# A decoder layer on one core: the second product's blocks begun together and its end split by token half, the fourth product in 256-column matmuls, the last block finished in halves

## The chip, the cores and the metric

One Trainium2 chip, one core of it. The metric is the device time of one execution of the whole kernel in microseconds (us), lower is better.

## The reference

One decoder layer on 256 tokens of width 2048, in float32:

```python
u = jnp.einsum('bsd,dc->bsc', x, w_in[l])                       # 1st product, 2048 -> 6160
conv_out = conformer_conv_group(u[..., :CONV_CH], ...)          # gated, depthwise conv of 31 taps, LayerNorm, silu
gdn_out = gated_deltanet_group(...)                             # 8 heads of 128, chunked delta rule, RMS norm, gate
mix = jnp.einsum('bsm,md->bsd', jnp.concatenate([conv_out, gdn_out], -1), w_out[l])   # 2nd, 2048 -> 2048
x = layer_norm(alpha * x + mix, ln1_g[l], ln1_b[l])
gu = jnp.einsum('bsd,df->bsf', x, w_gate_up[l])                 # 3rd product, 2048 -> 2 x 5632
hid = jax.nn.silu(gu[..., :D_FF]) * gu[..., D_FF:]
ffn = jnp.einsum('bsf,fd->bsd', hid, w_down[l])                 # 4th product, 5632 -> 2048
x = layer_norm(alpha * x + ffn, ln2_g[l], ln2_b[l])
```

## The kernel before

Every product is made on TensorE from float32 numbers split in a high part (`hi`, a copy in the fp32r format) and a low part (`lo`, the rest): three matmuls, hi x hi, hi x lo and lo x hi, are summed in PSUM. Weights come in chunks of 256 rows x 512 columns, 512 KB each. `wchunk` loads one on SyncE's queue into one of three `wraw` buffers (L92), ScalarE copies it to `whi` (L93) and VectorE subtracts to `wlo` (L100); there are four buffers of each kind. These three stand at a raised priority, so they run ahead of the rest. A scheduler orders the instructions of each engine by priority and readiness; each engine then runs its own list in order.

First product (`gemm_ws`, L206): 12 groups of 512 output features, 8 chunks each, weights stationary, 256 tokens moving: 24 matmuls of 256 columns a chunk. Between the chunks `tick` releases small steps of the convolution and of the delta rule, mostly fp32 matmuls and transposes, by due times in chunks; `EXTRA` corrects single due times. Their PSUM tiles come from the pool `sd` (4 banks, `ps`), those of the products from `mm` (4 banks, `mmt`).

Second product (`gemm2`, `tok_mm`): the activations are stationary, 128 x 128 at a time, and 512 weight columns move. There are four column blocks `nb`; a pass over the heads (`mixg`, pass 0) for all four, whose sums go into `y` (L747), then a pass over the convolution group (`mixc`, pass 1), whose sums `evac2` adds and takes statistics of (L753, L754). A block is 4 chunks x 2 tiles x 2 token halves (`tk`) x 3 matmuls. `require` runs what a chunk still needs: the second half of the heads, `head_mix(1)`, before the third chunk of a block of pass 0. Blocks 2 and 3 of pass 1 are done by token half: first `tk` 0 through eight chunks, then `tk` 1 through the same eight, held in `whi`/`wlo` (block 2) and `wxhi`/`wxlo` (block 3). After the first half come its statistics (`x1_stats`), its normalisation (`x1_norm`, four blocks `b`: L784 and L785 for `b` 0, L787 to L789 for the others) and the transposes into `x1` (`x1_turn`, L796, L800), which are put between matmuls of the second half by the list `X1T`.

Third product (L838, L847, L901): 22 groups of 8 chunks, weights stationary, 256 tokens moving. The first six chunks (`NF`, `first`; two in the buffers `fx...`) run with token half 0 alone (`fill`) while the second half is normalised and turned.

Fourth product (L940 on): as the second, four blocks of 22 chunks, 44 tiles, with `hid` stationary. In the last block six chunks are held back and done by token half; `evac4` adds and takes statistics of 512 columns (L929, L930), `finish` normalises (L936, L937) and sends 512 columns at a time (L938).

Pools lie one after the other in SBUF: `wp` with the weight buffers, `cp` with constants and statistics, `big` (`x_hi`, `x_lo`, `y`, `x1`), then the pools of the stages, with `mixc`, `mixg` and `hid`.

Of the kernel before, what the change touches and what calls it, by code (L numbers as in the profile page):

```python
# [60 lines left out]
def hybrid_layer(ctx: ExitStack, tc, xT, xn, w1, wba, w2, w3, w4, pvec, consts, hrow, lrow, out):  # L61
# [155 lines left out]
    def gates():  # L217
        wb = pb.tile([P, KT, P], F32R, tag="mixg", name="wb")
# [545 lines left out]
    for nb in range(2):  # L764
        banks = gemm2(1, nb)
# [11 lines left out]
    def x1_norm(tk, b, m, r, nmr):  # L777
        with tc.high_priority(offset=LPRI):
# [9 lines left out]
            TT(sl, sl, rows1[:, 0, bs], op=ALU.mult)  # L788
            return TT(sl, sl, rows1[:, 1, bs], op=ALU.add)  # L789
# [13 lines left out]
    for nb in (2, 3):  # L803
        for c in range(4):
            into = [pc.tile([P, 2, 512], F32R, tag=t, name=t, bufs=4) for t in ("wxhi", "wxlo")] if nb == 3 else None
            ws[nb, c] = wchunk(w2[1, nb, c], into=into)
    first = []
    for tk in range(2):
        for nb in (2, 3):
            if tk and nb == 3:  # L810
                for c in range(NF):
                    into = None
                    if c < NX:
                        into = [pc.tile([P, 2, 512], dt, tag=t, name=t, bufs=NX)
                                for t, dt in (("fxhi", F32R), ("fxlo", F32R), ("fxraw", F32))]
                    with tc.issue_after(loads[0].ins):
                        first.append(wload(w3[0, c], into=into))
            bank = mmt("g2t")
            for kt in range(8):
                tok_mm(bank, act_c, kt, tk, *ws[nb, kt // 2], kt % 2, 8)  # L820
                if tk and (nb, kt) in X1T:
                    with tc.issue_after(last[0].ins):
                        x1_turn(0, 4 * X1T.index((nb, kt)), 4)
            evac2(nb, tk, bank)
        sc1 = x1_stats(tk)
        hold = x1_norm(tk, 0, *sc1)
        if tk == 0:
            for b in range(1, 4):
                x1_norm(tk, b, *sc1)
# [23 lines left out]
    fill = [g3_hi(banks3, first[c][1], c, t0) for c in range(NF)]  # L853
# [65 lines left out]
    st2 = cp.tile([P, 2, 4, 6], F32, name="st2")  # L919
# [7 lines left out]
    def evac4(nb, tk, bank):  # L927
        sl = y[:, tk, nb * 512:nb * 512 + 512]
        STT(sl, sl, ALPHA, bank, op0=ALU.mult, op1=ALU.add)  # L929
        nc.vector.bn_stats(st2[:, tk, nb, :], sl)  # L930

    def finish(tk):
        m, r, _ = ln_scalars(st2[:, tk], f"b{tk}")
# [117 lines left out]
```

## Time and profile before

| what | us |
|---|---|
| median of 3 runs | 1171.71 |
| lowest, highest | 1171.03, 1172.68 |
| the profiled execution | 1173.28 |
| its span | 1171.5 |
| TensorE busy in the span | 1153.6 |
| VectorE, ScalarE, GpSimd busy | 735.6, 561.3, 34.9 |

The span runs from the first to the last instruction of one profiled execution. A matmul's busy time overlaps the next one's, so its spacing is read from start to start, or from how many fall into a stretch. In rows of a timeline "x2" merges two instructions; in a bracket stand the idle time of the engine before the row and the instruction that ended it.

### The profile page before, as it was taken

How to read it: one execution, taken by the hardware profiler on the slowest of the kernel's cores; microseconds unless marked ns; L12 is line 12 of the kernel's file. 1: busy time of each engine (PE TensorE's matmuls, PEld its weight loads, DVE VectorE, ACT ScalarE, POOL GpSimd, SP SyncE). 2: the span in 40 equal slices, each digit the busy share in tenths (PEclk: the TensorE clock that was granted, in tenths of full speed). 3: DMA queues.
4: the chain of work that ended last, by engine and by line, in shares of the span. 5: the costliest groups of instructions: out<-in, count | busy, mean ns of one | idle time of the engine just before them, and what ended most of it. 6: DMA issues, size and time to landing. Idle time of an engine off the chain costs nothing.

```text
span 1171.5 us, 20710 instructions
## 1 busy us (share of the span) xinstructions
PE 1153.6 (98%) x8514; PEld 1087.4 (93%) x8514; DVE 735.6 (63%) x1092; ACT 561.3 (48%) x803; POOL 34.9 (3%) x44
## 2 busy tenths in 40 slices
PE   9999999999999999999999999999999999999996
PEld 9999999999988879999999999999999888888884
DVE  5998998978847777545545455455554445454545
ACT  6567455556664544444444444444444333333340
POOL 1001011100000000000000000000000000000000
PEclk9999999999999999999999999999999999999998
DMA  8556564453535744655555555555555755555552
GB/s 292 182 190 214 176 210 156 153 196 127 198 129 177 263 150 159 217 191 192 197 195 191 194 195 197 191 191 196 197 194 192 264 187 190 197 189 189 197 202 86
DMA packets 62014, 222.65 MB, mean 190 GB/s; under 512 B 7168, under 2 KB 7680, under 8 KB 61280
## 3 DMA queue, kind: packets, MB, share of 16 engines
q1 hardware_dynamic: 58464, 208.37, 52.4%
q0 software_dynamic: 2160, 10.88, 2.8%
q10 hardware_dynamic: 1296, 2.10, 0.5%
q8 instruction: 66, 1.08, 0.4%
q14 instruction: 28, 0.23, 0.1%
HBM read 216.86 MB, written 4.46 MB: 189 GB/s over the span
## 4 chain that ended last, share of the span: by engine, by line
PE 71%; ACT 1%; DVE 1%; issue 1%; DMA 1%; POOL 0%; DVEq 0%; ACTq 0%
PE g3b L901 20%; PE g3a L901 20%; PE g4b L715 3%; PE g4a L715 3%; PE g4a L714 3%; PE g4b L714 3%; PE g4b L713 3%; PE g4a L713 3%; PE g1a L206 1%; PE g1b L206 1%; PE g2a L715 1%; PE g2a L713 1%; PE g2b L713 1%; PE g2a L714 1%; PE g2b L715 1%; PE g2b L714 1%
## 5 line engine op out<-in xcount | busy, mean ns | idle before, releaser
L100 DVE TENSOR_TENSOR wlo<-wraw,whi 128x1024 fp32r<-128x1024 f32 (+1 forms) x386 | 469.8, 1218 | 392.3 <-ACT whi L93 390.3
L93 ACT ACTIVATE whi<-wraw 128x1024 fp32r<-128x1024 f32 (+1 forms) x386 | 406.9, 1056 | 498.5 <-PE g3b L901 232.1
L901 PE MATMUL g3b<-x,whi 128*128 128x256 f32 x1344 | 261.7, 276 | 0.0
L901 PE MATMUL g3a<-x,whi 128*128 128x256 f32 x1344 | 261.6, 276 | 0.0
L901 PEld LDWEIGHTS g3a<-x,whi 128*128 128x128 f32 x1344 | 202.3, 188 | 0.0
L901 PEld LDWEIGHTS g3b<-x,whi 128*128 128x128 f32 x1344 | 202.3, 188 | 0.0
L901 PE MATMUL g3a<-x,wlo 128*128 128x256 f32 x672 | 130.8, 276 | 0.0
L901 PE MATMUL g3b<-x,wlo 128*128 128x256 f32 x672 | 130.8, 276 | 0.0
L639 DVE SCALAR_TENSOR_TENSOR cacc<-hh,pv,cacc 128x255 f32<-128x255 f32 (+27 forms) x240 | 100.8, 463 | 0.7 <-ACT cacc L636 0.7
L901 PEld LDWEIGHTS g3a<-x,wlo 128*128 128x128 f32 x672 | 101.2, 188 | 0.0
L901 PEld LDWEIGHTS g3b<-x,wlo 128*128 128x128 f32 x672 | 101.1, 188 | 0.0
L206 PE MATMUL g1a<-x_hi,whi 128*128 128x256 f32 x384 | 79.8, 290 | 0.9 <-ACT whi L93 0.5
L206 PE MATMUL g1b<-x_hi,whi 128*128 128x256 f32 x384 | 76.6, 281 | 0.0
L206 PE MATMUL g1a<-x_lo,whi 128*128 128x256 f32 x384 | 76.5, 281 | 0.0
L206 PE MATMUL g1b<-x_lo,whi 128*128 128x256 f32 x384 | 76.5, 281 | 0.0
L206 PE MATMUL g1a<-x_hi,wlo 128*128 128x256 f32 x384 | 76.4, 281 | 0.0
L206 PE MATMUL g1b<-x_hi,wlo 128*128 128x256 f32 x384 | 76.3, 280 | 0.0
L715 PE MATMUL g4b<-whi,hid 128*128 128x512 f32 x172 | 67.8, 394 | 0.0
L715 PE MATMUL g4a<-whi,hid 128*128 128x512 f32 x172 | 67.8, 394 | 0.0
L714 PE MATMUL g4a<-wlo,hid 128*128 128x512 f32 x172 | 67.4, 392 | 0.0
L714 PE MATMUL g4b<-wlo,hid 128*128 128x512 f32 x172 | 67.4, 392 | 0.0
L713 PE MATMUL g4a<-whi,hid 128*128 128x512 f32 x172 | 66.8, 388 | 0.0
(319 smaller groups left out, 1519.2 us busy)
## 6 DMA issues: line engine op xcount, KB each, us to landing
wraw<-in_w SPq DMA_DIRECT2D x388, 512.0 KB, 3.3
y<-in_xn POOLq DMA_DIRECT2D x1, 2048.0 KB, 8.5
rows<-in_lrow POOLq DMA_DIRECT2D x2, 1024.0 KB, 6.9
l<-in_lrow POOLq DMA_DIRECT2D x2, 1024.0 KB, 7.7
out<-y SPq DMA_DIRECT2D x8, 256.0 KB, 2.6
xr<-in_xT ACTq DMA_DIRECT2D x7, 256.0 KB, 5.4
wraw<-in_w SPq DMA_DIRECT2D x4, 256.0 KB, 4.1
dzx<-zbg POOLq DMA_DIRECT2D x2, 512.0 KB, 4.9
```

The source lines that it names most:

```text
L93: ACT(hi[:, k], raw[:, k], AF.Copy)
L100: TT(lo[:, k], raw[:, k], hi[:, k].bitcast(F32), op=ALU.subtract)
L206: last[0] = MM(o, lhsT=w[:, k2, ct * P:ct * P + P], rhs=r[:, kt, :], start=(kt == 0 and ct % 2 == 0 and r is r_hi and not fin), stop=(fin ...
L639: STT(a[:, s:], hh[:, i, :S - s], pcol(w + TAPS - 1 - s), a[:, s:], op0=ALU.mult, op1=ALU.add)
L713: MM(bank, lhsT=a_hi[:, tsl], rhs=hi[:, k2, :], start=(kt == 0), stop=False)
L714: MM(bank, lhsT=a_hi[:, tsl], rhs=lo[:, k2, :], start=False, stop=False)
L715: last[0] = MM(bank, lhsT=a_lo[:, tsl], rhs=hi[:, k2, :], start=False, stop=(kt == n - 1))
L901: last[0] = MM(banks[ct // 2][:, (ct % 2) * S:(ct % 2) * S + S], lhsT=w[:, k2, ct * P:ct * P + P], rhs=x1[kt // 8][:, kt % 8, part, :], st ...
```

## The change

In pass 0 of the second product three blocks do their first half together, then their second half, then block 3 follows; block 2 takes its two PSUM banks from `sd`. `head_mix(1)` gets a due time four chunks later. `pair_mm` takes the place of `tok_mm`: hi x hi in 512 columns, the other two parts in two matmuls of 256 columns each. In pass 1 the first two chunks of block 2 are done for both token halves; the six chunks of `LASTW` are done by token half. Two of the four turns of token half 0 go between the third product's first chunks. `x1_norm` of block 2 multiplies and adds on GpSimd. In the fourth product `half_mm` makes every matmul 256 columns wide; token half 1 is added, measured and, in the last block, finished in pieces of 256 columns. The statistics `st2` become one tile of 80 columns, 320 bytes where 192 stood; `wb` and `mixg` get 16 columns more, `mixg` uses its tile from column 16 on.

```diff
-        wb = pb.tile([P, KT, P], F32R, tag="mixg", name="wb")
+        wb = pb.tile([P, 4 * KT * P // 2 + 16], F32R, tag="mixg", name="wb")
+        wb = wb[:, 0:KT * P].rearrange("p (k n) -> p k n", k=KT)
-            mixb.append(pb.tile([P, 2, 8, S], F32R, tag="mixg", name="mixg"))
+            m = pb.tile([P, 4 * KT * P // 2 + 16], F32R, tag="mixg", name="mixg")
+            mixb.append(m[:, 16:].rearrange("p (a k n) -> p a k n", a=2, k=8))
+    def pair_mm(banks, act, c, tks, hi, lo, n):
+        for tk in tks:
+            tsl = slice(tk * P, tk * P + P)
+            for kt in (2 * c, 2 * c + 1):
+                MM(banks[tk], lhsT=act(kt)[0][:, tsl], rhs=hi[:, kt % 2, :], start=(kt == 0), stop=False,
+                   skip_group_check=True)
+        for part, w in ((0, lo), (1, hi)):
+            for kt in (2 * c, 2 * c + 1):
+                for hf in range(2):
+                    cs = slice(hf * 256, hf * 256 + 256)
+                    for tk in tks:
+                        last[0] = MM(banks[tk][:, cs], lhsT=act(kt)[part][:, tk * P:tk * P + P], rhs=w[:, kt % 2, cs],
+                                     start=False, stop=(part == 1 and kt == n - 1), skip_group_check=True)
+    def half_mm(banks, act, kts, tks, hfs, hi, lo, n):
+        for part, w in ((0, hi), (1, hi), (0, lo)):
+            for kt in kts:
+                for hf in hfs:
+                    cs = slice(hf * 256, hf * 256 + 256)
+                    for tk in tks:
+                        last[0] = MM(banks[tk][:, cs], lhsT=act(kt)[part][:, tk * P:tk * P + P], rhs=w[:, kt % 2, cs],
+                                     start=(kt == 0 and hf == 0 and part == 0 and w is hi),
+                                     stop=(w is lo and kt == n - 1), skip_group_check=True)
-    def gemm2(pas, nb):
...
+    def gemm2(pas, nbs):
+        banks = {}
+        for half in range(2):
+            for nb in nbs:
+                if half == 0:
+                    banks[nb] = [mmt("g2a"), mmt("g2b")] if nb < 2 or nb == 3 or pas else [ps("g2c"), ps("g2d")]
+                for c in (2 * half, 2 * half + 1):
+                    hi, lo = wchunk(w2[pas, nb, c])
+                    require(("gc"[pas], half))
+                    pair_mm(banks[nb], act_c if pas else act_g, c, (0, 1), hi, lo, 8)
+                    tick()
-    for nb in range(4):
...
+    for nbs in ((0, 1, 2), (3,)):
+        banks = gemm2(0, nbs)
+        for nb in nbs:
+            for tk in range(2):
+                ysl = y[:, tk, nb * 512:nb * 512 + 512]
+                STT(ysl, ysl, ALPHA, banks[nb][tk], op0=ALU.mult, op1=ALU.add)
-        with tc.high_priority(offset=2 * LPRI if tk and nb > 1 else LPRI if nb == 3 else 0):
+        with tc.high_priority(offset=2 * LPRI if nb > 1 else 0):
-        banks = gemm2(1, nb)
+        banks = gemm2(1, (nb,))[nb]
-            TT(sl, sl, rows1[:, 0, bs], op=ALU.mult)
-            return TT(sl, sl, rows1[:, 1, bs], op=ALU.add)
+            tt = nc.gpsimd.tensor_tensor if b == 2 else TT
+            tt(sl, sl, rows1[:, 0, bs], op=ALU.mult)
+            return tt(sl, sl, rows1[:, 1, bs], op=ALU.add)
-    for nb in (2, 3):
-        for c in range(4):
-            into = [pc.tile([P, 2, 512], F32R, tag=t, name=t, bufs=4) for t in ("wxhi", "wxlo")] if nb == 3 else None
-            ws[nb, c] = wchunk(w2[1, nb, c], into=into)
+    last_banks = {nb: [mmt("g2t"), mmt("g2u")] for nb in (2, 3)}
+    for c in range(2):
+        hi, lo = wchunk(w2[1, 2, c])
+        pair_mm(last_banks[2], act_c, c, (0, 1), hi, lo, 8)
+    for nb, c in LASTW:
+        into = [pc.tile([P, 2, 512], F32R, tag=t, name=t, bufs=4) for t in ("wxhi", "wxlo")] if nb == 3 else None
+        ws[nb, c] = wchunk(w2[1, nb, c], into=into)
-    for tk in range(2):
...
+    for nb, c in LASTW:
+        pair_mm(last_banks[nb], act_c, c, (0,), *ws[nb, c], 8)
+        if c == 3:
+            evac2(nb, 0, last_banks[nb][0])
+    sc1 = x1_stats(0)
+    for b in range(4):
+        x1_norm(0, b, *sc1)
+    turns = 0
+    for nb, c in sorted(LASTW):
+        if (nb, c) == (3, 0):
+            for i in range(NF):
+                into = None
+                if i < NX:
+                    into = [pc.tile([P, 2, 512], dt, tag=t, name=t, bufs=NX)
+                            for t, dt in (("fxhi", F32R), ("fxlo", F32R), ("fxraw", F32))]
+                with tc.issue_after(loads[0].ins):
+                    first.append(wload(w3[0, i], into=into))
+        pair_mm(last_banks[nb], act_c, c, (1,), *ws[nb, c], 8)
+        if (nb, c) in X1T:
+            with tc.issue_after(last[0].ins):
+                x1_turn(0, 4 * turns, 4)
+            turns += 1
+        if c == 3:
+            evac2(nb, 1, last_banks[nb][1])
+    sc1 = x1_stats(1)
+    hold = x1_norm(1, 0, *sc1)
-    fill = [g3_hi(banks3, first[c][1], c, t0) for c in range(NF)]
+    fill = []
+    for c in range(NF):
+        fill.append(g3_hi(banks3, first[c][1], c, t0))
+        if c in (1, 2):
+            with tc.issue_after(fill[c].ins):
+                x1_turn(0, 4 * c + 4, 4)
-    st2 = cp.tile([P, 2, 4, 6], F32, name="st2")
-    def evac4(nb, tk, bank):
...
+    HELD = 6
+    stb = cp.tile([P, 80], F32, name="st2")
+    st2 = [stb[:, 0:24].rearrange("p (a b) -> p a b", a=4), stb[:, 24:72].rearrange("p (a b) -> p a b", a=8)]
+    def evac4(nb, tk, bank, hfs=None):
+        for hf in hfs or (0, 1)[:tk + 1]:
+            n = 256 if tk else 512
+            sl = y[:, tk, nb * 512 + hf * n:nb * 512 + hf * n + n]
+            STT(sl, sl, ALPHA, bank[:, hf * n:hf * n + n], op0=ALU.mult, op1=ALU.add)
+            nc.vector.bn_stats(st2[tk][:, nb * (tk + 1) + hf, :], sl)
+    def finish(tk, edges):
+        m, r, _ = ln_scalars(st2[tk], f"b{tk}")
+        g2, b2 = (l2[:, i].rearrange("p a b -> p (a b)") for i in range(2))
+        for lo, up in zip(edges, edges[1:]):
+            sl = y[:, tk, lo:up]
+            STT(sl, sl, m, g2[:, lo:up], op0=ALU.subtract, op1=ALU.mult)
+            STT(sl, sl, r, b2[:, lo:up], op0=ALU.mult, op1=ALU.add)
+            nc.sync.dma_start(out[tk * P:tk * P + P, lo:up], sl)
-        held = 6 if nb == 3 else 0
+        held = HELD if nb == 3 else 0
-            for k2 in range(2):
-                for tk in range(2):
-                    tok_mm(banks[tk], act_h, 2 * c + k2, tk, hi, lo, k2, FT)
+            half_mm(banks, act_h, (2 * c, 2 * c + 1), (0, 1), (0, 1), hi, lo, FT)
+        if not held:
+            for tk in range(2):
+                evac4(nb, tk, banks[tk])
+            continue
-        for tk in range(2):
...
+        for tk, hfs in ((0, (0, 1)), (1, (0,)), (1, (1,))):
+            for c in range(NC4 - held, NC4):
+                half_mm(banks, act_h, (2 * c, 2 * c + 1), (tk,), hfs, *ws[c - NC4 + held], FT)
+            evac4(nb, tk, banks[tk], hfs if tk else None)
+            if tk == 0:
+                finish(0, (0, 512, 1024, 1536, 2048))
+    finish(1, (0, 512, 1024, 1536, 1792, 2048))
+-EXTRA = {..., 'head_mix_1': -3, ...}
+EXTRA = {..., 'head_mix_1': 1, ...}
-X1T = [(2, 7), (3, 2), (3, 4), (3, 7)]
+LASTW = [(2, 2), (3, 0), (2, 3), (3, 1), (3, 2), (3, 3)]
+X1T = [(3, 2), (3, 3)]
```

## Rows read from the trace of the kernel before

**Rows 1.** The page, part 1: busy time of each engine, share of the span.

```profile
PE 1153.6 (98%) x8514; PEld 1087.4 (93%) x8514; DVE 735.6 (63%) x1092; ACT 561.3 (48%) x803; POOL 34.9 (3%) x44
```

**Rows 2.** Table of stretches: us; busy us (count) of PE, PEld, DVE, ACT, POOL; clock; DMA; GB/s.

```profile
40.00:64.00 24.00, 24.00 (x206) 24.00 (x206) 24.00 (x74) 9.53 (x12) 0.00 (x0) 1.00 0.53 176
...
66.00:81.00 15.00, 15.00 (x134) 15.00 (x134) 15.00 (x32) 11.80 (x19) 0.00 (x0) 1.00 0.54 176
...
480.00:880.00 400.00, 400.00 (x3532) 400.00 (x3531) 202.90 (x185) 175.34 (x186) 0.00 (x0) 1.00 0.58 194
...
960.00:1120.00 160.00, 160.00 (x701) 131.29 (x700) 78.05 (x70) 62.12 (x59) 0.00 (x0) 1.00 0.56 191
```

**Rows 3.** Timeline of TensorE, third product's beginning: start, duration, engine, line, operation.

```profile
455.74 0.39 PE L838 MATMUL g3a<-x,whi 128*128 128x512 f32 x1
...
457.60 0.28 PE L847 MATMUL g3a<-x,wlo 128*128 128x256 f32 x1
...
458.51 0.39 PE L838 MATMUL g3a<-x,whi 128*128 128x512 f32 x1
```

**Rows 4.** Timeline of TensorE, head of the second product.

```profile
340.93 0.40 PE L713 MATMUL g2a<-whi,mixg 128*128 128x512 f32 x1
...
343.72 0.40 PE L713 MATMUL g2a<-whi,mixg 128*128 128x512 f32 x1
...
345.33 0.33 PE L615 MATMUL poT<-con,vs 128*128 128x128 f32 x1 [1.21 <-ACT vs L586]
```

**Rows 5.** Timeline of TensorE, end of the second product.

```profile
415.93 0.39 PE L715 MATMUL g2t<-wxhi,mixc 128*128 128x512 f32 x1
...
417.85 0.50 PE L713 MATMUL g2t<-wxhi,mixc 128*128 128x512 f32 x1 [1.53 <-ACT wxhi L93]
...
419.11 0.66 PE L714 MATMUL g2t<-wxlo,mixc 128*128 128x512 f32 x1 [0.76 <-DVE wxlo L100]
...
422.86 0.39 PE L713 MATMUL g2t<-wxhi,mixc 128*128 128x512 f32 x1
```

**Rows 6.** Table of stretches, two microseconds at the end of the second product.

```profile
420.00:422.00 2.00, 2.00 (x6) 1.61 (x5) 1.53 (x2) 1.34 (x2) 0.00 (x0) 0.50 0.93 303
```

**Rows 7.** Chain of waits, end of the second product: start us, us, what.

```profile
410.60 6.12 DMA wraw<-in_w
...
416.74 1.06 ACT wxhi L93
```

**Rows 8.** Timeline of VectorE, GpSimd and TensorE, turn from second to third product.

```profile
417.82 2.48 DVE L100 TENSOR_TENSOR wxlo<-wraw,wxhi 128x1024 fp32r<-128x1024 f32 x2 [2.23 <-ACT wxhi L93]
...
423.75 0.69 DVE L753 TENSOR_TENSOR y<-y,g2t 128x512 f32<-128x512 f32 x1 [2.21 <-PE g2t L715]
...
427.51 0.48 DVE L784 SCALAR_TENSOR_TENSOR y<-y,mva,rows 128x256 f32<-128x256 f32 x1
...
427.92 0.14 DVE L738 TENSOR_SCALAR ra<-mva 128x1 f32<-128x1 f32 x1
...
427.98 0.47 DVE L784 SCALAR_TENSOR_TENSOR y<-y,mva,rows 128x256 f32<-128x256 f32 x1
...
428.15 0.74 POOL L215 TENSOR_TENSOR ra<-ra,mhalf 128x1 f32<-128x1 f32 x1 [37.00 <-DVE ra L738]
...
429.46 0.44 PE L796 MATMUL px1T<-con,y 128*128 128x128 f32 x2 [0.24 <-DVE y L785]
...
430.99 1.88 DVE L788 TENSOR_TENSOR y<-y,rows 128x512 f32<-128x512 f32 x3
...
432.78 1.89 DVE L789 TENSOR_TENSOR y<-y,rows 128x512 f32<-128x512 f32 x3
```

**Rows 9.** Timeline of VectorE behind the last matmul.

```profile
1160.21 0.69 DVE L929 SCALAR_TENSOR_TENSOR y<-y,g4b 128x512 f32<-128x512 f32 x1 [1.09 <-PE g4b L715]
...
1160.94 0.69 DVE L930 BATCH_NORM_STATS2 st<-y 128x6 f32<-128x512 f32 x1
...
1161.67 0.26 DVE L736 BATCH_NORM_AGGREGATE mvb<-st 128x2 f32<-128x24 f32 x1
```

More of the change, by code (lines that the diff above doesn't have):

```diff
@@ L742, in hybrid_layer @@
     at(clock[0] + CLN, conv_ln)
-    for nb in range(4):
-        banks = gemm2(0, nb)
-        for tk in range(2):
-            ysl = y[:, tk, nb * 512:nb * 512 + 512]
-            STT(ysl, ysl, ALPHA, banks[tk], op0=ALU.mult, op1=ALU.add)
+    for nbs in ((0, 1, 2), (3,)):
[4 more added lines that the diff above has]
+                STT(ysl, ysl, ALPHA, banks[nb][tk], op0=ALU.mult, op1=ALU.add)
     st1 = cp.tile([P, 2, 4, 6], F32, name="st1")
@@ L802, in hybrid_layer @@
     ws = {}
-    for nb in (2, 3):
-        for c in range(4):
-            into = [pc.tile([P, 2, 512], F32R, tag=t, name=t, bufs=4) for t in ("wxhi", "wxlo")] if nb == 3 else None
-            ws[nb, c] = wchunk(w2[1, nb, c], into=into)
-    first = []
-    for tk in range(2):
[L809 to L829, printed above, removed]
@@ L925, in act_h @@
         return hid[:, 0, kt, :], hid[:, 1, kt, :]
-    def evac4(nb, tk, bank):
[L928 to L933, printed above, removed]
-        for nb in range(4):
-            sl = y[:, tk, nb * 512:nb * 512 + 512]
-            STT(sl, sl, m, l2[:, 0, nb, :], op0=ALU.subtract, op1=ALU.mult)
-            STT(sl, sl, r, l2[:, 1, nb, :], op0=ALU.mult, op1=ALU.add)
-            nc.sync.dma_start(out[tk * P:tk * P + P, nb * 512:nb * 512 + 512], sl)
-    NC4 = FT // 2
+    NC4 = FT // 2
+    HELD = 6
[15 more added lines that the diff above has]
+            nc.sync.dma_start(out[tk * P:tk * P + P, lo:up], sl)
     wx = big.tile([P, 2, 2, 2, 512], F32R, tag="big", name="wx")
@@ L953, in hybrid_layer @@
             ws.append(wchunk(w4[nb, c], into=(wx[:, i, 0], wx[:, i, 1]) if i < 2 else None))
-        for tk in range(2):
-            for kt in range(FT - 2 * held, FT):
-                tok_mm(banks[tk], act_h, kt, tk, *ws[kt // 2 - NC4 + held], kt % 2, FT)
-            evac4(nb, tk, banks[tk])
-            if held:
-                finish(tk)
-EXTRA = {'conv_ln3': 1, 'v_tok_4': 2, 'out2_0': 2, 'quad_local_1_1': 1, 'level_t_0_64': -3, 'out3_0': 1, 'level_b_0_32': 1, 'kq_tok_0': 2, 'quad_local_0_0': 1, 'gates': -1, 'out4_1': -1, 'level_t_1_64': 1, 'level_b_1_64': -3, 'kq_tok_2': -2, 'quad_local_1_2': 1, 'out3_1': -3, 'head_mix_1': -3, 'level_a_0_16': 1, 'level_a_0_64': 1, 'quad_local_0_2': 2, 'level_a_1_64': -1, 'kq_tok_4': 2, 'out2_1': 2, 'quad_local_1_3': 1}
+        for tk, hfs in ((0, (0, 1)), (1, (0,)), (1, (1,))):
[5 more added lines that the diff above has]
+    finish(1, (0, 512, 1024, 1536, 1792, 2048))
+EXTRA = {'conv_ln3': 1, 'v_tok_4': 2, 'out2_0': 2, 'quad_local_1_1': 1, 'level_t_0_64': -3, 'out3_0': 1, 'level_b_0_32': 1, 'kq_tok_0': 2, 'quad_local_0_0': 1, 'gates': -1, 'out4_1': -1, 'level_t_1_64': 1, 'level_b_1_64': -3, 'kq_tok_2': -2, 'quad_local_1_2': 1, 'out3_1': -3, 'head_mix_1': 1, 'level_a_0_16': 1, 'level_a_0_64': 1, 'quad_local_0_2': 2, 'level_a_1_64': -1, 'kq_tok_4': 2, 'out2_1': 2, 'quad_local_1_3': 1}
 NW = 8
```

7 lines of the change are left out of this document (removed).

## The prediction

> **What bounds the kernel now.** I read the page first. TensorE (PE) is busy 1153.6 of 1171.5 us [rows 1], so the time is the number of matmuls times their spacing, plus the few places where PE waits, plus the tail behind the last matmul. The rest is read in that order: the spacing from the table of stretches and from the timeline of PE, the waits from PE's timeline (the bracket behind a row is idle time and who ended it), each wait's cause from the chain of waits, and the tail from the timeline of all engines.
>
> The spacing. In the third product 3532 matmuls of 256 columns touch 400 us [rows 2]; two or three of them overlap the edges, so one starts every 113.3 ns. In the fourth, 701 of 512 columns touch 160 us: less two at the edges, 228.9 ns each. Two of the narrow ones would take 226.7 ns. The same operands in both widths stand side by side in [rows 3]: eight matmuls of 512 columns from 455.74 to 457.60 us, 232.5 ns each, then eight of 256 in 0.91 us, 113.8 each, so two halves take 228 ns. The 256-column form is not always that quick: in the first product 206 touch 24 us in one stretch (117.9 ns each, less the edges) and 134 touch 15 us in another (114) [rows 2]. I call them the slow and the fast spacing; they lie 4.5 ns apart for the same line, and which one holds lasts for tens of microseconds.
>
> **The change part by part.** The sum is made against the profiled execution, 1173.28 us, of which 1171.5 is the span; it lies 1.57 above the median of 1171.71, which I take the sum from.
>
> 1. Fourth product in 256 columns. It has 4 blocks x 44 tiles x 2 token halves x 3 = 1056 matmuls of 512 columns; they become 2112. At the fast spacing 2112 x 113.3 = 239.3 us against 1056 x 228.9 = 241.7: -2.4. At the slow spacing 2112 x 117.8 = 248.8: +7.1. No interleaved fp32 work stands in the fourth product, as none does in the third, which is fast throughout [rows 2], while the first product has it; so I take -2.4 and keep both ends. The weight copies hi and lo, 1.06 us on ScalarE and 1.24 (half of 2.48) on VectorE a chunk [rows 7, 8], are covered by 2.75 us of PE a chunk as before.
>
> A rule that speaks against this part: the Trainium skill, TensorE: Matmul & The Clock Gate, section "Back-to-back issue gap", gives a matmul a fixed 2.5 ns on top of its columns, so 1056 more of them would cost 2.6 us. The trace does not agree: two narrow ones take 226.7 to 228 ns, a wide one 228.9 to 232.5 [rows 2, 3]. It stays a rival.
>
> 2. Head of the second product. PE does twelve matmuls in 2.79 us (232.5 ns each) up to 343.72 and then the next only at 345.33, after 1.21 us idle for the normalisation of the second four heads [rows 4]; 1.61 less 0.23 is 1.4 us lost. The change puts the first half of three blocks, six chunks of 2.8 us, ahead of what needs those heads, where two stood before; `head_mix(1)` is due four chunks later. The wait is covered by four more chunks, 11 us: -1.4. The cover goes if the pair of banks that block 2 takes from the other pool holds up a late step of the heads or of the convolution's normalisation; then half comes back, -0.7.
>
> 3. The first pass, 64 (tile, half) pairs of three matmuls. 3 x 232.5 = 697.5 ns a pair [rows 4] become one of 512 and four of 256: 232.5 + 453.3 = 685.8. 64 x 11.7 ns: -0.75, which also is what the 64-byte shift of `mixg` can give. Small fp32 matmuls stand between these, so the slow spacing is possible: 64 x (4 x 4.5 - 11.7) = +0.4. In the second pass the matmuls stand at about 229 ns as in the fourth; one of 232.5 and four of 113.3 are 685.8 against 687: 0, and +1.1 if slow.
>
> 4. End of the second product. From 415.93 the next matmul starts at 417.85 and the one after at 419.11, each 0.23 us of work; 1.69 + 1.03 us are idle. Then nine take 3.75 us to 422.86 instead of 2.06 [rows 5]: the granted clock of 420 to 422 us is 0.50 [rows 6], the 1.2 GHz level, after PE had idled. 1.69 + 1.03 + 1.69 = 4.4 us. The chain says why: a chunk asked for at 410.60 needed 6.12 us, ScalarE then makes hi at 416.74 and VectorE lo from 417.82 [rows 7, 8]. PE had run through eight chunks with one token half each, 1.4 us a chunk. Now the first two chunks of block 2 are used for both halves (2.75 us each) before six are used by half. Counted from 407.9, the seventh chunk is wanted 2 x 2.75 + 4 x 1.39 = 11.1 us on, at 419.0 (its hi is there at 417.80), its lo 0.46 us later, at 419.4 (there at 419.05); the eighth at 420.4 and 420.8, there at 419.05 and 420.30. So it fits by some 0.4 us, if VectorE does not put something between. It may: block 2 of the first half ends at 417.5, and its add and statistics, 0.69 us each as the add in [rows 8], fall ahead of those two lo copies. I take 0.7 us back: -3.7. Bounds: -4.4, and -1.5 if a wait of that size lowers the clock again.
>
> 5. The turn to the third product. The turns of blocks 2 and 3 move behind the third product's first chunks; the cover of the second half's normalisation grows by them. For the first half less is left between: the first add at 423.75 leads to the first turn at 429.46 [rows 8], 5.7 us; the new order offers five chunks of 1.39 us, enough, and the 0.24 us of waiting there can go. The second turn needs block 1, whose add ends behind three multiplications (430.99, 1.88 us) and the first of three adds (432.78) [rows 8], about 433.4, 9.7 us after 423.75; it now stands some 9 us after. GpSimd takes one of the three multiplications and adds away, twice 0.62 us of VectorE [rows 8]. I charge +0.4; bounds -0.4, and +2.5 if each half loses about the 1.25 us that should be saved.
>
> No row shows a 512-column operation on GpSimd; the nearest is one of a single column, 0.74 us [rows 8]. Its block is wanted one chunk after block 1's, about 1 us and a turn later, so only a duration above some 2 us each would show; this lies within the +2.5. The Trainium skill, SBUF — State Buffer, section "SBUF: two separate sides", says that GpSimd and a two-input VectorE operation exclude each other for a whole instruction. By that VectorE would wait for GpSimd and gain nothing, and the term would be nearer to its upper end; no row here shows the two together.
>
> 6. The tail. The last add and its statistics take from 1160.21 to 1161.67, 1.46 us [rows 9]; on 256 columns each takes about 0.41 (one of 0.48 starts at 427.51 and the next operation 0.41 later, at 427.92 [rows 8]): 0.82. The half before it is covered: VectorE idles 1.09 us ahead of 1160.21 and is wanted for 0.82. One block in two halves costs 4 x 0.41 - 1.41 = +0.2, and the last transfer is half as large, at best -0.1. -0.5; bounds -0.7 and 0.
>
> 7. The padding. Statistics of 320 bytes stand where 192 stood, so every tile of the pools after it moves by 128 bytes; `wb` and `mixg` grow by 64. Nothing in the work depends on it, and I price it at 0. But no row tells what chooses between slow and fast spacing, so first and third product may change over: rivals below.
>
> Sum: -2.4 - 1.4 - 0.75 + 0 - 3.7 + 0.4 - 0.5 = -8.35. From 1171.7: 1163.4 us. With the bounds of parts 2 to 6 the forecast's own range is 1160.5 to 1168.
>
> **The rivals.**
> Third product slow (the one on the other side). The tiles move against the weight buffers, which stand in an earlier pool and do not move. If that puts the third product at the slow spacing, its 4032 matmuls (21 groups of 8 chunks of 24) cost 4.5 ns more, +18.1: 1181.5 us, slower. It decides from about half of them on, 8.35 / 0.0045 = 1860 matmuls. For it: 117.9 ns in the first product with the same form [rows 2]. Against: 400 us without a single change.
> Fourth product slow: +7.1 for -2.4, 1172.9, no change. For it, the same; against, no fp32 work in between.
> The end of the second product still starves: the margin is 0.4 us, and VectorE's order is not mine to see. 1163.4 + 3.7 = 1167.1.
> First product fast: of 39 us in [rows 2] 24 are slow; 2304 matmuls (12 groups of 192) x 24/39 x 4.5 ns = 6.4: 1157.0. The padding could do that as well as the contrary.
> A price for each start of a matmul: the rows compare a narrow and a wide form with weights stationary; in the fourth product the activations are stationary. If there a start costs as much as [rows 2] let me hope to save, 2.3 ns, the part is +2.4 for -2.4: 1168.2. By the figure on the skill's page (TensorE: Matmul & The Clock Gate), an estimate, it would be +2.6 and 1168.4.
>
> **How the numbers follow.** Chances: forecast 0.53, still starving 0.13, fourth slow 0.12, third slow 0.10, first fast 0.08, fixed price 0.04. The predicted time is the forecast's, 1163.4. Left out of 1155.5 to 1173.0 are the third slow (0.10), some of the fourth slow with a poor end of the second product (0.05) and the best of the first fast (0.03). A measurement of this kernel tells about 0.2%, 2.3 us, from no change. Faster: 0.53 + 0.13 + 0.08 + 0.04, less a little for bad ends, 0.77; same: most of the fourth slow, 0.08; slower: the third slow and 0.05 of the others, 0.15.
>
> **What the profile after would show.** The fourth product with 2112 matmuls at 113.3 ns (mean duration 276, not 281). No idle time of PE at the second half of the heads. Six chunks at the end of the second product without a wait above 0.5 us and with the granted clock at 2.4 GHz. VectorE's last add and statistics at half length. First and third product at the same mean durations as before. I am wrong if any stretch of 256 columns that now stands at 276 ns shows 281, or if GpSimd's two operations are what PE's first turns wait for.

## The result and the profile after

The changed kernel takes 1190.99 us (median of three executions, 1190.83 to 1191.67) where the kernel before takes 1171.37 in the same comparison: a ratio of 1.0174, 95% interval 1.0160 to 1.0187. It is slower by 19.6 us; the forecast was 1163.4, and its range ended at 1173.0.

A fourth execution, the profiled one, took 1440.49 us at a mean granted clock of 0.75 and is left out (with it the median is 1191.33), so the profile shown is of another execution of the same kernel, in run e1. That one took 1208.1 us: in it the third product too ran at the slow spacing, and the other executions lie some 18 us below it.

The page of after (run e1, as for all rows of after in this section), part 1 (as [rows 1]):

```profile
PE 1182.5 (98%) x9826; PEld 1171.7 (97%) x9826; DVE 738.1 (61%) x1098; ACT 560.9 (47%) x803; POOL 42.2 (3%) x48
```

TensorE (PE) is as full as before: the time is again the matmuls' spacing and the places where PE waits. The stretches of [rows 2], and the head of the second product [rows 4], in the same view of after:

```profile
40.00:64.00 24.00, 24.00 (x206) 24.00 (x205) 24.00 (x73) 10.27 (x12) 0.00 (x0) 1.00 0.54 167
66.00:81.00 15.00, 15.00 (x130) 15.00 (x130) 15.00 (x34) 12.21 (x19) 0.00 (x0) 1.00 0.60 182
480.00:880.00 400.00, 400.00 (x3399) 400.00 (x3398) 195.04 (x178) 167.91 (x178) 0.00 (x0) 1.00 0.60 187
960.00:1120.00 160.00, 160.00 (x1361) 160.00 (x1360) 74.70 (x69) 59.49 (x57) 0.00 (x0) 1.00 0.60 188
...
340.00:346.00 6.00, 6.00 (x47) 5.64 (x46) 1.99 (x3) 5.04 (x19) 0.09 (x1) 1.00 0.28 87
```

The fourth product's 1361 narrow matmuls in 160 us are one every 117.7 ns (less two at the edges, as in the prediction), the slow spacing; the third product's 3399 in 400 us are one every 117.8, for 3532 and 113.3 before. At the head of the second product PE is busy without a break.

The end of the second product and the turn, in the same view. [Rows 6] had a clock of 0.50 here, and PE idle [rows 5]; now it is full up to nearly 430 and idle behind that, and the clock is 0.59 from 435 to 440:

```profile
415.00:420.00 5.00, 5.00 (x40) 4.75 (x39) 3.76 (x5) 3.01 (x3) 0.00 (x0) 1.00 0.89 320
420.00:425.00 5.00, 5.00 (x37) 4.66 (x37) 4.01 (x5) 3.36 (x4) 0.00 (x0) 1.00 0.96 371
425.00:430.00 5.00, 4.79 (x36) 4.33 (x35) 4.53 (x9) 2.13 (x2) 0.67 (x1) 1.00 0.43 137
430.00:435.00 5.00, 2.63 (x17) 2.11 (x18) 3.94 (x8) 3.74 (x5) 1.14 (x2) 1.00 0.01 3
435.00:440.00 5.00, 1.72 (x9) 1.48 (x8) 4.93 (x6) 0.62 (x2) 2.30 (x2) 0.59 0.00 0
440.00:445.00 5.00, 5.00 (x35) 5.00 (x34) 3.19 (x9) 1.11 (x2) 0.73 (x1) 0.72 0.00 0
```

Who PE waits for there (timeline of PE; the matmuls without a bracket are left out):

```profile
430.64 0.44 PE L826 MATMUL px1T<-con,y 128*128 128x128 f32 x2 [0.85 <-DVE y L814]
431.63 0.44 PE L826 MATMUL px1T<-con,y 128*128 128x128 f32 x2 [0.55 <-DVE y L814]
...
434.64 0.66 PE L826 MATMUL px1T<-con,y 128*128 128x128 f32 x4 [1.18 <-DVE y L819]
438.58 0.58 PE L875 MATMUL g3a<-x,fxhi 128*128 128x256 f32 x1 [3.28 <-DVE x L830]
```

All four end with VectorE's normalisation of the first token half and the low half of its first turn. Later, at a turn of the second half, PE also waits for GpSimd:

```profile
452.85 0.66 PE L826 MATMUL px1T<-con,y 128*128 128x128 f32 x4 [0.75 <-POOL y L819]
```

The timeline of VectorE shows what it did ahead of and during the first four waits (as [rows 8]):

```profile
418.91 2.52 DVE L100 TENSOR_TENSOR wxlo<-wraw,wxhi 128x1024 fp32r<-128x1024 f32 x2 [1.24 <-ACT wxhi L93]
422.35 1.22 DVE L100 TENSOR_TENSOR fxlo<-fxraw,fxhi 128x1024 fp32r<-128x1024 f32 x1 [0.91 <-ACT fxhi L93]
423.49 0.68 DVE L782 TENSOR_TENSOR y<-y,g2t 128x512 f32<-128x512 f32 x1
424.09 1.22 DVE L100 TENSOR_TENSOR fxlo<-fxraw,fxhi 128x1024 fp32r<-128x1024 f32 x1
...
425.83 1.21 DVE L100 TENSOR_TENSOR wlo<-wraw,whi 128x1024 fp32r<-128x1024 f32 x1
426.95 0.68 DVE L782 TENSOR_TENSOR y<-y,g2t 128x512 f32<-128x512 f32 x1
...
428.39 0.26 DVE L764 BATCH_NORM_AGGREGATE mva<-st 128x2 f32<-128x24 f32 x1
...
433.17 0.69 DVE L818 TENSOR_TENSOR y<-y,rows 128x512 f32<-128x512 f32 x1 [0.93 <-ACT y L816]
...
434.58 1.68 DVE L818 TENSOR_TENSOR y<-y,rows 128x512 f32<-128x512 f32 x1
436.29 1.63 DVE L819 TENSOR_TENSOR y<-y,rows 128x512 f32<-128x512 f32 x1
437.85 0.68 DVE L830 TENSOR_TENSOR x<-px1T,x 128x512 fp32r<-128x512 f32 x1
```

and the timeline of GpSimd its two new operations for the first token half:

```profile
433.92 1.79 POOL L818 TENSOR_TENSOR y<-y,rows 128x512 f32<-128x512 f32 x1 [3.86 <-ACT y L816]
435.79 1.59 POOL L819 TENSOR_TENSOR y<-y,rows 128x512 f32<-128x512 f32 x1
```

The end of the fourth product (timeline of VectorE and PE, as [rows 9]):

```profile
1188.64 1.41 DVE L986 SCALAR_TENSOR_TENSOR y<-y,rb,l 128x512 f32<-128x512 f32 x2
1189.97 0.41 DVE L977 SCALAR_TENSOR_TENSOR y<-y,g4b 128x256 f32<-128x256 f32 x1
1190.44 2.93 PE L739 MATMUL g4b<-wx,hid 128*128 128x256 f32 x12 [3.47 <-DVE y L977]
...
1196.36 0.42 DVE L977 SCALAR_TENSOR_TENSOR y<-y,g4b 128x256 f32<-128x256 f32 x1 [5.51 <-PE g4b L739]
1196.82 0.43 DVE L978 BATCH_NORM_STATS2 st<-y 128x6 f32<-128x256 f32 x1
```

The last add and statistics are short, as foreseen; but the second column half waits 3.47 us for the add of the first half, which stands behind `finish(0)`, and the clock falls behind the wait (table of stretches, PE alone: us, busy, clock, DMA, GB/s):

```profile
1190.00:1195.00 5.00, 4.56 (x26) 0.66 0.30 108
```

The stages of five kernels, one profiled execution each (after is the one of 1208.1), read from the timelines of PE (us). A stage runs from the start of its first matmul to the start of the next stage's first; the turn is counted from the start of the second product's last matmul, and the last row from the start of the fourth's last:

| stage | before | after | e2 | e6 | e12 |
|---|---|---|---|---|---|
| first product and all before it | 334.2 | 336.9 | 335.1 | 335.6 | 335.2 |
| second product, heads | 51.7 | 50.0 | 50.3 | 50.2 | 50.2 |
| convolution group, blocks 0 and 1 | 22.0 | 22.0 | 22.2 | 22.2 | 22.2 |
| blocks 2 and 3 | 28.1 | 24.2 | 23.4 | 24.3 | 22.6 |
| turn: to the third product's second group | 25.3 | 34.5 | 34.3 | 32.9 | 29.0 |
| rest of the third product | 457.0 | 474.9 | 457.0 | 457.0 | 457.0 |
| fourth product | 241.5 | 253.5 | 246.3 | 240.0 | 240.0 |
| behind the last matmul | 11.7 | 10.3 | 10.3 | 10.8 | 10.8 |
| span | 1171.5 | 1206.3 | 1178.9 | 1172.8 | 1166.9 |

The first row differs by 2.2 us between e6 and e8 (335.6, 337.8), whose code is the same up to there, so nothing is concluded from differences of that size in it. Blocks 2 and 3 vary too: with their code as in before they took 28.1 us there and in e3, but 26.0 in e10 and 24.9 in e14. And two of the four turns, about 0.35 us of PE each, count to blocks 2 and 3 in before and to the turn in the changed kernels.

### The profile page after: what moved, and what is told of

Its sections match the earlier page's. It is cut to its first block, busy times and chain, and to the rows that moved or that the text cites. A ratio compares the mean times of both kernels' runs of the same rounds, so it can differ in the third digit from the quotient of the medians.

```text
span 1438.7 us, 23347 instructions
## 1 busy us (share of the span) xinstructions
PE 1423.7 (99%) x9826; PEld 1406.7 (98%) x9826; DVE 745.1 (52%) x1098; ACT 563.4 (39%) x803; POOL 42.3 (3%) x48
## 5 line engine op out<-in xcount | busy, mean ns | idle before, releaser
L943 PE MATMUL g3b<-x,whi 128*128 128x256 f32 x1344 | 306.0, 313 | 0.0
L943 PE MATMUL g3a<-x,whi 128*128 128x256 f32 x1344 | 305.9, 313 | 0.0
L943 PEld LDWEIGHTS g3b<-x,whi 128*128 128x128 f32 x1344 | 245.4, 223 | 0.0
L943 PEld LDWEIGHTS g3a<-x,whi 128*128 128x128 f32 x1344 | 245.4, 223 | 0.0
L739 PE MATMUL g4b<-whi,hid 128*128 128x256 f32 x688 | 194.6, 314 | 0.0
L739 PE MATMUL g4a<-whi,hid 128*128 128x256 f32 x688 | 193.8, 314 | 0.0
L739 PEld LDWEIGHTS g4b<-whi,hid 128*128 128x128 f32 x688 | 152.1, 224 | 0.0
L739 PEld LDWEIGHTS g4a<-whi,hid 128*128 128x128 f32 x688 | 151.7, 224 | 0.0
L739 PE MATMUL g4b<-wlo,hid 128*128 128x256 f32 x344 | 99.1, 313 | 0.0
L739 PE MATMUL g4a<-wlo,hid 128*128 128x256 f32 x344 | 98.4, 313 | 0.0
```

Of the source, the lines that this page charges most:

```text
L739: last[0] = MM(banks[tk][:, cs], lhsT=act(kt)[part][:, tk * P:tk * P + P], rhs=w[:, kt % 2, cs], start=(kt == 0 and hf == 0 and part == 0 ...
L943: last[0] = MM(banks[ct // 2][:, (ct % 2) * S:(ct % 2) * S + S], lhsT=w[:, k2, ct * P:ct * P + P], rhs=x1[kt // 8][:, kt % 8, part, :], st ...
```

## The experiments

**Where the tiles lie.** The statistics tile `st2`, grown from 192 to 320 bytes, moves every tile behind it, the activations among them, by 128 bytes against the weight buffers of `wp`. One run of the changed kernel again, one of it with 448 bytes, one of before with 320:

```diff
-    stb = cp.tile([P, 80], F32, name="st2")      # after: 320 bytes
+    stb = cp.tile([P, 112], F32, name="st2")     # e2: 448
-    st2 = cp.tile([P, 2, 4, 6], F32, name="st2") # before: 192
+    stb = cp.tile([P, 80], F32, name="st2")      # e3: 320
```

> The changed kernel once more, for a profile at the full granted clock. Theory A (the 128-byte move of the tiles against the weight buffers puts products at the slow spacing): the third product at a mean matmul duration of 281 ns instead of 276 and 117.8 ns from start to start, +18 us, and the fourth at 117.8 ns, +7 us against before; the waits of the second product gone, -5 us; together 1191 us. Theory B (what stands ahead of the third product, its new turns, puts it at the slow spacing; the place of the tiles is of no account): the same spacings, so this run alone doesn't tell A from B. Theory C (the loss lies in the second product or in waits of the turn): third and fourth product at 113.3 ns and 20 us of idle time of TensorE between 330 and 470 us.

> The changed kernel with 112 columns of statistics instead of 80: every later tile lies 256 bytes behind where the kernel before had it, instead of 128; nothing else differs. Theory A, if the place counts modulo 256 bytes: the third product is back at 113.3 ns, -18 us; the fourth either stays slow (1173 us) or comes back too (1163 us). Theory B: no difference, 1191 us. Theory C: no difference, 1191 us.

> The kernel before with the 320-byte tile for the statistics of the end and nothing else of the change: every later tile moves by 128 bytes. Theory A: the third product at 117.8 ns, +18 us, 1189 us, with a few us more or less where the first product's share of slow spacing changes. Theory B: 1171 us, third product at 113.3 ns. Theory C: 1171 us.

Measured: e1 1208.1 and 1189.38; e2 1179.19, ratio 1.0060 (1.0039 to 1.0080); e3 1177.37 without one execution at 1194.94, ratio 1.0053 (1.0032 to 1.0073). So 128 bytes more give the changed kernel some 12 us back (11.8 at the medians), and the same 128 bytes alone cost the kernel before some 6. Theories B and C had expected no difference from the place alone, and fell. Theory A had expected 1189 for e3; but its third product stayed fast in the profile, and only the fourth became slower, 160/686 = 233 ns a wide matmul for 228.9. In e2 both are at the fast spacing (same view as [rows 2], first e2, then e3):

```profile
480.00:880.00 400.00, 400.00 (x3531) 400.00 (x3531) 201.91 (x184) 174.68 (x184) 0.00 (x0) 1.00 0.62 194
960.00:1120.00 160.00, 160.00 (x1414) 160.00 (x1413) 79.69 (x77) 62.26 (x59) 0.00 (x0) 1.00 0.62 194
```

```profile
480.00:880.00 400.00, 400.00 (x3531) 400.00 (x3531) 202.26 (x184) 174.65 (x185) 0.00 (x0) 1.00 0.61 195
960.00:1120.00 160.00, 160.00 (x688) 128.90 (x687) 76.84 (x70) 60.43 (x57) 0.00 (x0) 1.00 0.58 187
```

Two more places for the kernel before, 64 and 192 bytes further:

```diff
+    stb = cp.tile([P, 64], F32, name="st2")      # e13: 256 bytes
+    stb = cp.tile([P, 96], F32, name="st2")      # e14: 384 bytes
```

> Kernel: before, with the statistics tile of 256 bytes for 192, so that everything behind it lies 64 bytes further (e3_before_pad128: 128 bytes further, +6.2 us; e2_after_pad256 against after: 256 bytes are as good as none). If only one place of the four in 256 bytes is good, the one that before happens to have: fourth product 246 us, first product 1 to 3 us longer, 1176 to 1180. If the bad place is one of four: fourth 241.5, 1170 to 1173.

> Kernel: as e13_before_pad64, with 384 bytes, 192 bytes further. If only the place of before is good: 1176 to 1180, with the fourth product at 246 us. If the bad place is the one at 128 bytes alone: 1170 to 1173.

Measured: e13 1202.71, ratio 1.0276 (1.0259 to 1.0292); e14 1200.39, ratio 1.0256 (1.0242 to 1.0270). Of the four places within 256 bytes the one of before is the only good one for the whole; the cost is more than three times what was expected, and most of it lies in the third product (with the turn 509.6 us in e13 for 482.3). In e13 the first product is longer too, 340.9 us for 334.2. First e13, then e14:

```profile
480.00:880.00 400.00, 400.00 (x3335) 400.00 (x3335) 190.72 (x173) 164.12 (x173) 0.00 (x0) 1.00 0.56 184
960.00:1120.00 160.00, 160.00 (x708) 132.53 (x706) 76.50 (x68) 62.60 (x59) 0.00 (x0) 1.00 0.59 193
```

```profile
480.00:880.00 400.00, 400.00 (x3373) 400.00 (x3372) 194.08 (x177) 166.87 (x177) 0.00 (x0) 1.00 0.57 186
960.00:1120.00 160.00, 160.00 (x690) 129.74 (x689) 75.06 (x66) 60.46 (x57) 0.00 (x0) 1.00 0.57 189
```

3335 and 3373 matmuls in 400 us, less two, are 120.0 and 118.7 ns each. The fourth product of e13 has its best spacing of all, 160/706 = 226.6 ns a wide matmul (239.2 us): what suits one product doesn't suit the other.

**GpSimd's share and the bank.** From here on all kernels but e7 have a good place: e2's, or, in e10, that of before.

```diff
-            tt = nc.gpsimd.tensor_tensor if b == 2 else TT   # e4, e6, e7
+            tt = TT
-        banks = [mmt("g4a"), mmt("g4b")]                     # e5, e6, e7
+        banks = [mmt("g4a"), mmt("g4b")] + ([ps("g4c")] if nb == 3 else [])
...
+                        own = len(banks) > 2 and tk == 1 and hf == 1
+                        last[0] = MM(banks[2 if own else tk][:, cs], lhsT=act(kt)[part][:, tk * P:tk * P + P],
...
-    stb = cp.tile([P, 112], F32, name="st2")                 # e7
+    stb = cp.tile([P, 80], F32, name="st2")
```

> As e2_after_pad256 (the changed kernel with the tiles 256 bytes on), but block 2 of the normalisation is multiplied and added on VectorE again, not on GpSimd. Theory D (while GpSimd runs its 1.6 to 2.1 us operations VectorE's two-input operations are held, and the low halves of the first turns queue behind them): the 34.3 us from the end of the second product to the third's second group fall to 25 or 26, no wait of 3 us ahead of the first matmul of the third product, 1170 us. Rival E (the new order of the turns is what is late, GpSimd is of no account): a wait of some 3 us stays, 1177 to 1180 us, since VectorE has 2.6 us more to do.

> As e2_after_pad256, but in the last block of the fourth product the second half of token half 1 is summed in a PSUM bank of its own, so that its matmuls need not wait until VectorE has read the first half out of the same bank. Theory F (TensorE waits for the first half's add, which stands behind the whole normalisation of token half 0, and then runs at 1.2 GHz for some us): no wait of 3.6 us near 1158, the fourth product takes 239 to 240 us instead of 246.3, 1172 to 1173 us. Rival G (the wait is for the weights that are held back): the wait stays, 1179 us.

> e4 and e5 together. Theories D and F: the gains add up, 1163 us, 8 us faster than the kernel before. If one of them only moves its wait elsewhere: 1170 us or more.

> e6 with the changed kernel's own 80 columns of statistics: tiles 128 bytes on instead of 256. Theory A (the place of the tiles modulo 256 bytes sets the spacing of the products whose weights lie in the first pool): fourth product at 117.8 ns, +9 us, first product +2 us, third product slow in some executions, +18 us: 1174 us, single executions at 1192. If the place is of no account when no waits stand ahead: 1163 us as e6.

Measured: e4 1177.48 (ratio 1.0055, 1.0041 to 1.0069), 1.7 below e2, but its interval lies within e2's. Theory D fell: the wait ahead of the third product is 2.95 us for 3.29. e5 1173.85 (1.0021, 1.0012 to 1.0030), 5.3 below e2: the fourth product takes 240.0 us for 246.3, PE's wait is gone, and the clock stays at its upper level (view as [rows 2]):

```profile
1155.00:1160.00 5.00, 5.00 (x45) 5.00 (x44) 4.93 (x10) 0.00 (x0) 0.99 (x1) 1.00 0.18 67
```

Rival G fell with it. The same change of the bank from e4 to e6, in one comparison, gives 3.8. e6 1173.69 (1.0015, 1.0006 to 1.0024): 1163 had been expected, since the waits of the turn were put down to GpSimd; they stayed, and the turn takes 32.9 us for 34.3. Against e5, in the same comparison, GpSimd's share makes 0.2 us: nothing that can be told from noise. e7 1182.88 (1.0099, 1.0085 to 1.0112): the place costs 9.2 us, of which the fourth product takes 8.3 (248.3 for 240.0).

**The turn.** In e6 PE ends the first token half at 422.0, 1.7 us earlier than the add at 423.75 shows for before, yet VectorE begins to normalise it at 427.71, where before began at 427.51 [rows 8]. Three low copies for the third product's first chunks, read only in its second pass, stand between. e8 changes only what follows (the low half of turn 0 ahead of blocks 2 and 3), e9 only the copies, e12 both:

```diff
-    early_lo = {c: wrest(first[c])[1] for c in range(NF - 3)}
+    early_lo = {}                                       # e9, e12
+    for c in range(NF - 3):
+        with tc.issue_after(n0.ins if c == 2 else hold.ins):
+            early_lo[c] = wrest(first[c])[1]
...
-            TT(sl, sl, rows1[:, 0, bs], op=ALU.mult)
-            return TT(sl, sl, rows1[:, 1, bs], op=ALU.add)
+            with tc.issue_after(after.ins) if after else ExitStack():   # e8, e12: blocks 2, 3
+                TT(sl, sl, rows1[:, 0, bs], op=ALU.mult)                # after the low half of turn 0
+                return TT(sl, sl, rows1[:, 1, bs], op=ALU.add)
...
```

> Kernel: the one of e6_both, with one order changed on VectorE: the multiplications and additions of blocks 2 and 3 of the first token half are issued behind the low half of turn 0 instead of ahead of it. Theory H (PE's longest wait in the turn, 2.95 us ahead of the first matmul of the third product in e6_both, ends with that low half, which stands on VectorE behind 3.1 us of work for blocks 2 and 3, although its source was there at 434.05): the low half moves from 436.5 to about 434.1, the wait falls to about 0.5, the turn from 32.9 to 30 to 31 us, and the time to 1170.5 to 1171.5. Theory G (the normalisation as a whole starts too late, since its statistics stand behind copies for the third product, and what is moved within it only moves the wait to the next turn): the turn falls by less than 1 us, 1173 to 1174.

> Kernel: the one of e6_both, with the low copies of the third product's first three weight chunks (3.6 us on VectorE, read late, in the second pass over the fill) issued later: that of chunk 2 behind the first block's normalisation, those of chunks 0 and 1 behind the second half's. Theory G (the step that failed in part 5: PE ends the first token half at 422.1 in e6_both, 1.6 us earlier than before, but VectorE's last statistics of that half come at 426.68, as late as before, since an add of block 2 that could start at 419.8 waits behind a copy whose source lands at 421.3 and two more copies stand in between): the aggregation moves from 427.4 to about 423.7, PE's waits ahead of the turns (0.66, 0.55, 1.18) and ahead of the third product (2.95) shrink to under 1 us in sum, the clock stays at 2.4 GHz, the turn falls from 32.9 to 25 to 27 us, and the time from 1173.7 to 1166 to 1168. Theory H (only the order among the low halves counts): the wait ahead of the third product stays, the turn falls by less than 2 us, 1172 to 1174.

> Kernel: both orders of VectorE changed at once, as e8_low_first and e9_copies_late: the three low copies of the third product's first chunks later, and the low half of turn 0 ahead of the multiplications of blocks 2 and 3. If the two are two causes one behind the other (theory G for the waits ahead of the turns, theory H for the 2.09 us ahead of the third product that e9_copies_late still shows): the wait ahead of the third product falls to 0.5 us or less, the clock there stays at 2.4 GHz, the turn falls from 29.8 to 27 to 28 us, and the time from 1170.8 to 1168 to 1169, the fastest of all. If something third holds the turn (the multiplications of the second half, or ScalarE): 1170 to 1171.5.

Measured: e8 1173.61 (ratio 1.0009, 1.0001 to 1.0018), 0.0006 below e6's ratio, with intervals that overlap: the long wait went from 2.95 to 0.51 us, as foreseen, but 0.93, 0.60 and 0.27 us came up at the next turns, and the turn fell by 2.3 us, as theory H has it, of which the time shows hardly anything. e9 1170.77 (0.9985, 0.9975 to 0.9995), ratio 0.0030 below e6. Its timeline of VectorE, then PE's only wait in it:

```profile
421.52 0.68 DVE L784 TENSOR_TENSOR y<-y,g2t 128x512 f32<-128x512 f32 x1
...
423.55 0.69 DVE L784 TENSOR_TENSOR y<-y,g2t 128x512 f32<-128x512 f32 x1 [0.62 <-PE g2t L730]
424.27 0.69 DVE L785 BATCH_NORM_STATS2 st<-y 128x6 f32<-128x512 f32 x1
425.00 0.27 DVE L766 BATCH_NORM_AGGREGATE mva<-st 128x2 f32<-128x24 f32 x1
...
434.11 0.68 DVE L832 TENSOR_TENSOR x<-px1T,x 128x512 fp32r<-128x512 f32 x1
```

```profile
434.85 0.39 PE L878 MATMUL g3a<-x,fxhi 128*128 128x256 f32 x1 [2.09 <-DVE x L832]
```

The second add now starts as soon as PE is done, the three waits ahead of the turns are gone, and the aggregation comes 1.5 us behind the end of PE's last matmul for it (423.5), where e6 had it 5.4 behind (422.0 to 427.41). The wait for the low half remains, and with it a granted clock of 0.66 from 435 to 440 us. Theory G had put too much on this: the turn fell to 29.8, not to 26. e12, both, 1168.65 (0.9982, 0.9973 to 0.9991): the waits left in its turn are

```profile
433.61 0.63 PE L828 MATMUL px1T<-con,y 128*128 128x128 f32 x4 [0.86 <-DVE y L821]
434.84 0.39 PE L881 MATMUL g3a<-x,whi 128*128 128x256 f32 x1 [0.60 <-DVE x L832]
...
437.69 0.39 PE L881 MATMUL g3a<-x,whi 128*128 128x256 f32 x1 [0.29 <-DVE x L832]
...
440.89 0.39 PE L881 MATMUL g3a<-x,fxhi 128*128 128x256 f32 x1 [0.62 <-DVE x L832]
```

2.4 us in sum, and the clock stays at 2.4 GHz. It has the lowest ratio here, 0.18% below before; its interval overlaps those of e9 and of e11 below.

**One part at a time.** e10 is before with the fourth product in 256 columns alone; e11 is e6 with the end of the second product and the turn as before.

```diff
...
-                    tok_mm(banks[tk], act_h, 2 * c + k2, tk, hi, lo, k2, FT)   # e10
+            half_mm(banks, act_h, (2 * c, 2 * c + 1), (0, 1), (0, 1), hi, lo, FT)
...
-LASTW = [(2, 2), (3, 0), (2, 3), (3, 1), (3, 2), (3, 3)]                       # e11
-X1T = [(3, 2), (3, 3)]
+X1T = [(2, 7), (3, 2), (3, 4), (3, 7)]
```

> Kernel: before, with the fourth product's matmuls in 256 columns and nothing else of the change (statistics, placement, second product, end of the kernel as before). Part 1 of the prediction put at this: 2112 matmuls at 113.3 ns, -2.4 us, 1169.0 to 1169.4. From the stage of e5_own_bank (fourth 240.0 us where before takes 241.5): -1.5, 1170. If a narrow matmul has a price of its own here (+2.4): 1174.

> Kernel: the one of e6_both, with the end of the second product and the turn as they were before (eight chunks by token half, four turns inside the second half); what stays of the change is the head of the second product, the fourth product in 256 columns and its end in halves, with an own bank. If the new end is worth less than nothing, as the stages say (28.1 + 25.3 us before, 24.3 + 32.9 in e6_both): -3.8 from 1173.7, 1169.5 to 1170.5, which is 1 to 2 us below before. If the early end of the second product does help behind (rival): 1173 or more.

Measured: e10 1171.81 against 1172.76, ratio 0.9994 (0.9983 to 1.0005); its fourth product takes 240.0 us for 241.5. e11 1171.15, ratio 0.9990 (0.9980 to 1.0000), 0.0025 below e6: the new end with its order on VectorE cost about 3 us more than the old one (in the profiles 57.2 us for 52.3, blocks 2 and 3 and the turn together). Whether the new end in e12's order beats the old one is not shown: 0.9982 and 0.9990 have intervals that overlap, and the two stages take 51.6 us in e12 where the old code took 51.3 (e10) to 53.4 (before).

## Why the prediction was wrong

At the medians the 19.6 us are: 11.8 for the place (after to e2), 5.3 for the bank (e2 to e5; 3.8 from e4 to e6), and 2.5 for the rest, in which a turn that lost 9 us stands against all that was gained. The forecast's own range was added up wrongly too: the bounds of parts 2 to 6 make 1161.7 to 1171.1, not 1160.5 to 1168. The result lies outside both.

**The padding, part 7, at 0: the largest error.** "Nothing in the work depends on it" is what failed. The place of the tiles behind `st2` chooses the spacing. With it fell the reason given in part 1 for the fast one, that no fp32 work stands in between: the fourth product of after and the third of e1, e13 and e14 are slow without such work. The rivals named it: the fourth product slow (+7.1 foreseen, 248.3 against 241.5 in e7) is what happens in after, and the third slow (+18.1 foreseen) is what happens in the one execution of 1208.1. I gave the two a chance of 0.22 together. The 11.8 is more than the 8.3 of the fourth product that e7 shows; in the profiles of e1 and e2 the first product too is longer by 1.8 us, which is within what that row varies by, and what the other 3 to 4 us are was not settled.

**The tail, part 6, at -0.5.** The tail itself did better, 11.7 to 10.3 (10.8 in e6 and e12). What failed is "the half before it is covered". It looked at VectorE's idle time ahead of [rows 9], and not at who waits for that add: PE wants to write the second half into the same bank, and the add stands on VectorE behind the normalisation of the first token half (1184.67 to 1190.0). 3.47 us of waiting and a granted clock of 0.66 from 1190 to 1195 us are the cost, and an own bank takes 5.3 us back (e5; 3.8 from e4 to e6).

**The turn, part 5, at +0.4 with an upper bound of +2.5; it was +9.0 (e2), of which some 0.7 are the two turns that moved into it.** Two steps failed. First, the 5.7 us from PE's end to the first turn were carried along with PE's earlier end. They don't move with it: VectorE's queue holds the copies of the third product at the same time as before, and so PE's gain at the end of the second product only became a wait at the turn. Shown by e9 and e12, where the copies come later. Second, I counted up to the turns, and not from a turn to its low half, which the third product reads: with blocks 2 and 3 in between on VectorE it came 3 us late. e8 moves that alone and gains little, e12 both; the turn is 29.0 there, and 2.4 us of waiting is left of it. For GpSimd I looked at its duration (up to 2 us; in the first half it took 1.59 and 1.79) and not at VectorE's: two-input operations there took 1.68 and 1.63 beside it, and 0.69 without. Both of the long ones end 0.55 us behind the GpSimd operation beside them (436.26 and 437.92, GpSimd's at 435.71 and 437.38). The Trainium skill, SBUF — State Buffer, "SBUF: two separate sides", says that a GpSimd operation which reads SBUF and a VectorE operation with two SBUF inputs exclude each other, and the rows agree; I had quoted it and left it within the bound. So GpSimd gained nothing. What it cost is not clear: taking its share back gave 1.7 us from e2 to e4 and 0.2 from e5 to e6, and the long waits stayed.

**The end of the second product, part 4, at -3.7: right as a mechanism.** 28.1 to 24.2 us, without a wait for weights and at full clock; 22.6 in e12. The size fits this one execution of before: the same code took 24.9 to 28.1 in other profiles, and some 0.7 of the difference are the turns that moved. The rival that it still starves fell.

**The head, part 2, at -1.4: right,** 51.7 to 50.0 us with part 3 in it. Part 3, at -0.75 and 0, came out between its bounds, at about nothing: the narrow matmuls of the second product last 279 ns in the good place too (e12), between 276 at the fast and 281 at the slow spacing, so that the heads gain only what part 2 gives, and blocks 0 and 1 lose 0.2.

**The fourth product in 256 columns, part 1, at -2.4.** In the good place -1.5, on its own not told from no change (e10). 240.0/2112 is 113.6 ns, where I took 113.3 from the third product. A price per matmul start, +2.4 as a rival, isn't seen: e10's 1056 further starts made the product shorter, 240.0 us for 241.5. The Trainium skill (TensorE: Matmul & The Clock Gate, "Back-to-back issue gap") has 2.5 ns in its formula for an isolated matmul, and says itself that a stream of them is spaced otherwise, so it was no rule for this product.

## What to carry to other kernels

A faster TensorE stage is worth something only if the engine that hands its result on is free then: follow the queue of that engine past the end of the stage, and move copies that are read late behind the chain. Before splitting a block in halves, ask who waits for the bank of the first half. And never call a change of a tile's size free: compare the spacing of untouched matmuls in both traces first; here 64 bytes cost 32 us.

## What the runs showed of the hardware

The spacing of matmuls depends on where the tiles behind `st2`, the activations among them, lie while the weight buffers of `wp` stand still, counted within 256 bytes. A shift of 256 is as good as none: the fourth product in 256 columns takes 240.0 us at either (e10, e5), the rest of the third 457.0 (before, e2). The three shifts between are not. From the rows of 480 to 880 and 960 to 1120 us of before, e13, e3 and e14, in ns a matmul:

| shift of the activations | third product, 256 columns | fourth, 512 columns | time against before |
|---|---|---|---|
| 0 | 113.3 | 228.9 | |
| 64 bytes | 120.0 | 226.6 | +31.9 |
| 128 bytes | 113.3 (117.8 in e1's profile of the changed kernel) | 233.2 | +6.0 |
| 192 bytes | 118.7 | 232.6 | +29.6 |

At 128 bytes the third product has either spacing, and the same kernel takes 1190 or 1208.1 us: e1's profile of 1208.1 shows 117.8 ns, those of e3 and e7 show 113.3. The execution of e3 at 1194.94 has no profile; that it is the same is inferred from its time. Whether the distance from the weights or the tiles' own address counts, which operands decide, and by what rule, wasn't tried; in the third product the weights are stationary and the activations move, in the fourth it is the other way round, and their best places differ.
